# A two-layer hybrid decoder step on one core: the first half of the tokens goes through the output projection and four feed-forward tiles inside the first mixer's scan

## The chip, the cores and the metric

One NeuronCore of a Trainium2 chip. The metric is the device time of one execution in microseconds (us), the median of several runs. PE is TensorE (matmuls), PEld its weight loads, DVE VectorE, ACT ScalarE, POOL GpSimd, SP the queue that issues nearly all DMAs.

## The reference, cut to what matters

544 tokens (512 of one prompt and 8 short sequences of 4) pass two layers of width 1024. Layer 0 has two mixers side by side, an RG-LRU (a gated linear recurrence) and an RWKV-7 time mixing (a matrix state per head, updated token by token); layer 1 has HGRN2. Behind each stands a feed-forward block.

```
p = rmsnorm(x) @ w_in_ab
out_a = gelu(p[gate]) * rg_lru(conv(p[u]))
S = S*w_t - (S kk_t)(kk_t a_t)^T + v_t k_t^T      # for each token, each of 8 heads
o_t = S r_t;  out_b = (groupnorm(o) + bonus) * g
x = x + concat(out_a, out_b) @ w_out_ab
xf = rmsnorm(x)
x = x + (silu(xf @ ffn_gate) * (xf @ ffn_up)) @ ffn_down
```

## The kernel before, in words

Activations lie transposed: 128 features on the partitions, the 544 tokens along the row. A product in float32 is made of three matmuls in a shorter format (fp32r): the high part of the weight by the high part of the activation, high by low, and low by high. So each weight block of 128 x 512 is loaded (`wf`, 256 KB), its high part copied by ACT (`wh`, L202) and its low part subtracted by DVE or POOL (`wl`, L205). `weights` (L196 on) does this from pools of 2 `wf` and 3 `wh`/`wl` buffers. One output column of 128 features needs 8 k-tiles, so 2 blocks and 24 matmuls for a half of 272 tokens (`dense_steps`), and both halves use the blocks while they are there.

Mixer 0 ends with the scan of the RWKV part: 16 chunks of 32 tokens, each a chain of three small groups of products (tile `ch`): the state by W, copied out by DVE (`rhs`, L827); that by the inverse Yt, copied out by four DVE instructions into the two Z tiles (L842); these by TM, added to the decayed state by DVE (L850); then the chunk's outputs (`ops`). Between the three groups `fill(HOP[i])` takes a number of steps from a list of generators, `self.work`: a step is one dense matmul. The list holds `recurrent()`, the four RG-LRU column pairs with their gates (tile `gate`), and later `lead(3)`, which begins the output projection of three columns for tokens 0 to 255 (`SPLIT`). `PLAN` is an order written by hand: `c` one chunk, `s` one step of the sample group (tiles rpss, opss, dpss), `g`/`h` the two halves of a groupnorm of 128 tokens, `l` the lead, `f` n fill steps, `d` empty the list. The scheduler of the language keeps this order by priorities: the chain is put first (`first()`), weights 400 places early; within an engine everything then runs in the order built.

After the scan `out_proj0` finishes the output projection, five columns in a mixed order with the weights kept in two extra pools (`wo`, `wo2`), three columns in the common way; then `ffn(0, ...)` runs 22 tiles of gate and up in groups of 8, 8 and 6, each followed by the 8 down columns of its group. The eighth input of the projection, `oa[3]`, is the last that the recurrent part delivers.

Of the kernel before, what the change touches and what calls it, by code (L numbers as in the profile page):

```python
# [20 lines left out]
D = 1024  # L21
KT = 8
# [14 lines left out]
WC = 4  # L37
FREE = 'r3'
# [90 lines left out]
class Build:  # L129
    def __init__(self, nc, tc, ins, outs, dbg=None):  # L130
# [10 lines left out]
        self.normed = set()  # L141

# [192 lines left out]
    def mixer0(self):  # L335
# [22 lines left out]
        kp = self.open("keep", side="right")  # L358
# [81 lines left out]
        Zt = m0.tile([128, NCH, 2, CH], F32, name="Zt")  # L440
        NTt = m0.tile([128, 2, NCH, CH], F32, name="NTt")
# [23 lines left out]
        def proj_begin(j):  # L465
            X = m0.tile([128, SEQ + 7 * NB + 3], F32, tag="X", name="X", bufs=XB)
# [6 lines left out]
        def proj_end(j, out, X):  # L473
            nc.gpsimd.tensor_copy(shift_sb[:, j, :], X[:, SEQ:NT + 1:4])
            d = m0.tile([128, SEQ + 7 * NB], F32, tag="d", name="d", bufs=DB)[:, :NT]
# [329 lines left out]
        def scan():  # L805
# [15 lines left out]
            for c in range(NCH):  # L821
# [13 lines left out]
                with first():  # L835
# [3 lines left out]
                    for e in range(2):  # L839
                        for par in range(2):  # L840
                            q = quad(par, e)
                            nc.vector.tensor_copy(zc[par][q, e::2], cu[q])  # L842
# [23 lines left out]
        def groupnorm(o, n, blk):  # L866
            assert self.gated
            self.normed.add(blk)
            with tc.high_priority(offset=GN_PRIO):
                yield from normalise(o, n, blk)  # L870

# [116 lines left out]
        def rglru(i, before):  # L988
            UX = m0.tile([128, SEQ + 7 * NB + 3], F32, tag="X", name="UX", bufs=XB)
# [19 lines left out]
            cf = m0.tile([128, NX], F32, tag="d", name="cf", bufs=DB)  # L1009
# [8 lines left out]
            gg = m0.tile([128, SEQ + 7 * NB], F32, tag="d", name="gg", bufs=DB)[:, :NT]  # L1018
# [49 lines left out]
        cat, ww0, ps0 = [], [], []  # L1068
        H0, H1 = slice(0, SPLIT), slice(SPLIT, NT)

        def lead(n):
            assert {0, 1} <= self.normed
            wo = (self.open("wo", side="right"), (2, 2 * n - 2))
            cat.extend(actp.tile([128, 2, NT], F32R, tag="a", name="cat") for _ in range(8))
            for j in range(3):
                self.hilo(cat[j], oa[j])
            for j in range(4):
                self.hilo(cat[3 + j], bon[j], H0)
            for m in range(n):
                ww0.append(self.column(I["w_out_ab"][m], 0, KT, wo if m else None))  # L1080
            for m in range(n):
# [606 lines left out]
```

## Time and profile before

| what | value |
|---|---|
| median of 3 runs | 1540.75 us (1539.14 to 1542.7) |
| the profiled execution | 1541.22 us, its span 1539.4 us |
| PE busy | 1465.2 us, 95% of the span, 13872 matmul records |
| DVE, ACT, POOL busy | 860.2, 552.5, 418.3 us |
| DMA | 133.86 MB |

A row of a timeline is: start, duration in us, engine, line, operation, output<-input, shapes, count, and in brackets how long the engine stood idle before it and what ended that. A row of waits is: who, waited for whom, total us, times, longest. PEclk is the granted clock of TensorE as a share of full speed. The times of the trace count from the start of the span.

### The profile page before, as it was taken

To read this page: it belongs to the slowest core of one execution; us is meant where nothing else is said; L and a number is where in the kernel's file an instruction comes from. 1 tells how busy PE (TensorE), PEld (TensorE's weight loads), DVE (VectorE), ACT (ScalarE), POOL (GpSimd) and SP (SyncE) were. 2 spreads that over 40 slices of the span, in tenths; PEclk is the share of its full clock that TensorE was granted. 3 is DMA by queue.
4 is the path that set the end of the run, shared out by engine and by line. 5 is a ranking of instruction groups with operands and counts; after the bars stand their busy time and mean duration, and the time that the engine had idled before them with its cause. 6 is when DMAs were issued, how large, how long until landed. Compare 5 with 4: busy or idle time off the path is not lost.

```text
span 1539.4 us, 33537 instructions
## 1 busy us (share of the span) xinstructions
PE 1465.2 (95%) x13872; PEld 1408.7 (92%) x13872; DVE 860.2 (56%) x1618; ACT 552.5 (36%) x997; POOL 418.3 (27%) x540
## 2 busy tenths in 40 slices
PE   6967888779999999999999999999999999999998
PEld 6857777669999999999999999999999999999997
DVE  7777555785544344334576667666674433444444
ACT  5634234354433233223352333333453322332224
POOL 3664535542110011001133434444431100110010
PEclk9978989889999999999999999999999999999999
DMA  4224311122232322322231232322242222223221
GB/s 158 70 71 104 105 38 36 49 80 93 83 96 83 90 89 84 96 83 91 85 120 58 85 98 85 106 87 90 97 124 90 89 86 87 90 90 90 84 75 59
DMA packets 92010, 133.86 MB, mean 87 GB/s; under 512 B 28976, under 2 KB 34864, under 8 KB 91728
## 3 DMA queue, kind: packets, MB, share of 16 engines
q1 hardware_dynamic: 91856, 131.71, 27.2%
q8 instruction: 109, 1.79, 0.5%
q14 instruction: 45, 0.37, 0.1%
HBM read 120.65 MB, written 11.02 MB: 86 GB/s over the span
## 4 chain that ended last, share of the span: by engine, by line
PE 84%; DVE 7%; ACT 3%; issue 2%; DMA 2%; POOL 1%; SPq 1%; DVEq 0%; POOLq 0%; ACTq 0%
PE acc L171 74%; PE lv L171 2%; PE ops L171 1%; PE ch L171 1%; DVE Z L842 1%; DVE t L571 0%; PE ds L171 0%; PE tr L1503 0%; DVE W L528 0%; PE nps L171 0%; DVE wl L205 0%; DMA S<-rS 0%; DMA x<-xT 0%; DMA wd<-down 0%; DVE Pd L653 0%
## 5 line engine op out<-in xcount | busy, mean ns | idle before, releaser
L171 PE MATMUL acc<-xg,wh 128*128 128x272 f32 x4544 | 888.1, 293 | 11.7 <-ACT xg L262 7.2
L171 PEld LDWEIGHTS acc<-xg,wh 128*128 128x128 f32 x4544 | 721.7, 191 | 21.7 <-ACT xg L262 7.5
L171 PE MATMUL acc<-xg,wl 128*128 128x272 f32 x2272 | 653.1, 293 | 0.2 <-DVE wl L205 0.2
L202 ACT ACTIVATE wh<-wf 128x512 fp32r<-128x512 f32 (+1 forms) x404 | 250.8, 621 | 655.8 <-PE acc L171 544.3
L171 PEld LDWEIGHTS acc<-xg,wl 128*128 128x128 f32 x2272 | 429.1, 190 | 4.9 <-issue 1.3
L205 DVE TENSOR_TENSOR wl<-wf,wh 128x512 fp32r<-128x512 f32 (+1 forms) x373 | 267.1, 716 | 192.2 <-ACT wh L202 166.2
L1207 POOL TENSOR_TENSOR S<-S,rstd 128x272 f32<-128x272 f32 x88 | 74.3, 845 | 645.3 <-ACT S L1206 645.2
L171 PE MATMUL acc<-h,wh 128*128 128x272 f32 x1280 | 236.9, 288 | 0.0
L171 PEld LDWEIGHTS acc<-h,wh 128*128 128x128 f32 x1280 | 198.0, 188 | 0.0
L171 PE MATMUL acc<-h,wl 128*128 128x272 f32 x640 | 176.7, 287 | 0.0
L171 PEld LDWEIGHTS acc<-h,wl 128*128 128x128 f32 x640 | 118.1, 188 | 0.0
L1210 DVE TENSOR_TENSOR hh<-acc,S 128x272 f32<-128x272 f32 x88 | 38.9, 442 | 127.2 <-PE acc L171 125.3
L171 PE MATMUL acc<-cat,wh 128*128 128x272 f32 (+2 forms) x512 | 100.2, 295 | 2.7 <-ACT wh L202 2.7
L171 PEld LDWEIGHTS acc<-cat,wh 128*128 128x128 f32 x512 | 82.7, 194 | 3.5 <-ACT wh L202 3.1
L1206 ACT ACTIVATE S<-t 128x272 f32<-128x272 f32 x88 | 37.8, 431 | 123.4 <-DVE t L1205 123.4
L1227 DVE TENSOR_TENSOR x<-acc,x 128x272 f32<-128x272 f32 x80 | 35.0, 439 | 83.3 <-PE acc L171 83.0
L1205 DVE TENSOR_TENSOR t<-acc,rstd 128x272 f32<-128x272 f32 x88 | 38.7, 441 | 70.7 <-PE acc L171 70.6
L171 PE MATMUL acc<-cat,wl 128*128 128x272 f32 (+2 forms) x256 | 74.2, 296 | 2.0 <-POOL wl L205 1.0
L280 POOL TENSOR_TENSOR ssq<-ssq,sq 128x544 f32<-128x544 f32 x33 | 46.5, 1410 | 93.4 <-ACT sq L279 93.0
L1477 POOL TENSOR_TENSOR K<-K,G 128x256 f32<-128x256 f32 (+1 forms) x48 | 39.8, 828 | 78.3 <-PE lv L171 78.3
L205 POOL TENSOR_TENSOR wl<-wf,wh 128x512 fp32r<-128x512 f32 x31 | 41.3, 1334 | 40.7 <-ACT wh L202 40.4
L171 PEld LDWEIGHTS acc<-cat,wl 128*128 128x128 f32 x256 | 49.2, 194 | 2.8 <-POOL wl L205 1.4
(341 smaller groups left out, 1506.9 us busy)
## 6 DMA issues: line engine op xcount, KB each, us to landing
wf<-gate SPq DMA_DIRECT2D x88, 256.0 KB
wf<-up SPq DMA_DIRECT2D x88, 256.0 KB
wf<-down SPq DMA_DIRECT2D x72, 256.0 KB
wf<-w_in_c SPq DMA_DIRECT2D x64, 256.0 KB
wf<-w_in_ab SPq DMA_DIRECT2D x44, 256.0 KB
x<-xT SPq DMA_DIRECT2D x16, 272.0 KB
wf<-w_out_ab SPq DMA_DIRECT2D x16, 256.0 KB
S<-hS SPq DMA_DIRECT2D x8, 512.0 KB
```

What stands on the lines that cost most here:

```text
L171: return self.seq(self.nc.tensor.matmul(out, lhsT, rhs, start=start, stop=stop, skip_group_check=True), chain)
L202: nc.scalar.activation(wh[:, :n], wf[:, :n], AF.Copy)
L205: eng.tensor_tensor(wl[:, :n], wf[:, :n], wh[:, :n].bitcast(F32), OP.subtract)
L280: eng.tensor_tensor(self.ssq, self.ssq, t, OP.add)
L842: nc.vector.tensor_copy(zc[par][q, e::2], cu[q])
L1205: nc.vector.tensor_tensor(t[:, c], ps, rs()[:, c], OP.mult)
L1206: nc.scalar.activation(S[:, c], t[:, c], AF.Silu)
L1207: nc.gpsimd.tensor_tensor(S[:, c], S[:, c], rs()[:, c], OP.mult)
L1210: nc.vector.tensor_tensor(hh[:, c], ps, S[:, c], OP.mult)
L1227: nc.vector.tensor_tensor(x[:, c], ps, x[:, c], OP.add)
L1477: PTT(kv[:, :, 0], kv[:, :, 0], g2[:, :, 1, None].to_broadcast([128, m, b]), OP.mult)
```

## The change

The first half of the tokens (0 to 255) now goes as fill work through the whole output projection and the first four of the 22 feed-forward tiles (`PAIRS`), in `first_half()`, which joins the list after the eleventh chunk. Its first two columns (`EARLY`) leave out the last k-tile until `oa[3]` is there. What is not done by the end of the scan is done in `d0`, before the second half of the last groupnorm. `second_half` then takes tokens 256 to 543 through the same projection and the same four tiles, with all these weights loaded again, and from there both halves together. The weight loads outside the first two columns go in turn through the old pool (3 of 5) and a new one, `h0` (2 of 5), with 1 `wf` and 2 `wh`/`wl` buffers. The down products run in two groups (12 and 10 tiles) instead of three. Of the chain's four copies two go to ACT. Every second `wl` subtraction in the scan (it was every one) is POOL's. The sample group's steps and the groupnorms have other places in `PLAN`.

```diff
-LO = (3, 1)
+LO = (3, 2)
-PLAN = 's1 f30 c1 c1 s1 c1 s1 c1 s1 c1 s1 g0 c1 s1 c1 s1 c1 h0 s1 c1 s1 c1 s1 s1 c1 c1 s1 g1 c1 s1 c1 s1 c1 h1 g2 s1 c1 s1 l3 c1 c1 h2 f20 d0'
+PLAN = 's1 f30 c1 c1 s1 s1 c1 s1 s1 c1 s1 c1 s1 g0 s1 c1 s1 c1 s1 h0 c1 s1 c1 s1 g1 c1 s1 s1 c1 h1 s1 s1 c1 l0 c1 g2 c1 c1 c1 h2 c1 g3 c1 d0 h3'
-HOP = (8, 7, 7)
+HOP = (9, 10, 9)
...
     def column(self, src, k0, kn, pool=None):
-        return [(k, self.weights(src, k0 + k, min(WC, kn - k), pool)) for k in range(0, kn, WC)]
+        out = []
+        for k in range(0, kn, WC):
+            own = pool
+            if self.h0 and own is None:
+                self.turn += 1
+                if self.turn % 5 < 2:
+                    own = (self.h0, (1, 2))
+            out.append((k, self.weights(src, k0 + k, min(WC, kn - k), own)))
+        return out
...
                             q = quad(par, e)
-                            nc.vector.tensor_copy(zc[par][q, e::2], cu[q])
+                            copy(e, zc[par][q, e::2], cu[q])
...
+        def first_half():
             assert {0, 1} <= self.normed
+            self.close("rg", "join")
+            hp = self.h0 = self.open("h0", side="right")
+            cat = half["cat"] = [actp.tile([128, 2, NT], F32R, tag="a", name="cat") for _ in range(8)]
+            for j, src in enumerate([*oa[:3], *bon, oa[3]]):
+                self.hilo(cat[j], src, H0)
+            xs = half["x"] = [hp.tile([128, SPLIT], F32, name=f"xh{m}") for m in range(KT)]
+            for m in range(KT):
+                nc.sync.dma_start(xs[m], I["xT"][:, m, H0])
...
+            early = [(self.column(I["w_out_ab"][m], 0, KT, (self.wp, self.wbufs)), self.bank()) for m in range(EARLY)]
+            for ww, ps in early:
+                yield from self.run(None, acts, None, ww=ww, ps=ps, ks=range(KT - 1))
+            for m in range(KT):
...
+                if m < EARLY:
+                    yield from self.run(None, acts, ev, ww=early[m][0], ps=early[m][1], ks=(KT - 1,))
+                else:
+                    yield from self.run(I["w_out_ab"][m], acts, ev)
+                xg.append(self.scaled_half(hp, x, "ln_ffn0", m, ssq, SPLIT))
+            rs = half["rs"] = self.rstd_half(hp, ssq, SPLIT)
+            half["h"] = []
+            for ft in range(PAIRS):
+                yield from self.gate_up(hp, ft, [xg], [rs], half["h"])
...
+    def gate_up(self, hp, ft, xgs, rss, out, pool=None):
...
+        wg = self.column(self.i["gate0"][ft], 0, KT)
+        for c, xg, rs in zip(cuts, xgs, rss):
+            def evg(ps):
+                nc.vector.tensor_tensor(t[:, c], ps, rs(), OP.mult)
+                nc.scalar.activation(S[:, c], t[:, c], AF.Silu)
+                nc.gpsimd.tensor_tensor(S[:, c], S[:, c], rs(), OP.mult)
+            yield from self.run(None, [(a[:, 0], a[:, 1]) for a in xg], evg, ww=wg)
+        wu = self.column(self.i["up0"][ft], 0, KT)
...
+    def second_half(self, half):
...
+        for m in range(KT):
+            x = self.x[m][:, H1]
...
+            go(self.run(I["w_out_ab"][m], acts, ev))
+            xg1.append(self.scaled_half(hp, x, "ln_ffn0", m, ssq, n1))
+        rs1 = self.rstd_half(hp, ssq, n1)
+        h1 = []
+        for ft in range(PAIRS):
+            go(self.gate_up(hp, ft, [xg1], [rs1], h1))
...
+        for last, kn, pool in ((False, PAIRS + 8, self.act_a), (True, FT - PAIRS - 8, None)):
+            full = []
+            for ft in range(k0 + len(hs), k0 + kn):
+                own = self.act_a if last and len(full) < LENT else pool
+                go(self.gate_up(hp, ft, [half["xg"], xg1], [half["rs"], rs1], full, own))
```

Where instructions stand now, at three places. On PE, the fill between the first and the second product of a chunk (`acc` is a dense product, `xg` the recurrent part's input, `cat` the projection's, `rhs` by `Yt` the second product), before:

```order
L171 MATMUL jps<-join,Zt 32x16 x32
L171 MATMUL acc<-xg,wh 128x272
L171 MATMUL acc<-xg,wl 128x272
L171 MATMUL acc<-xg,wh 128x272 x2
L171 MATMUL acc<-xg,wl 128x272
L171 MATMUL acc<-xg,wh 128x272 x2
L171 MATMUL acc<-xg,wl 128x272
L171 MATMUL ch<-rhs,Yt 32x64 x8
```

and in the fourteenth chunk of the changed kernel:

```order
L176 MATMUL ch<-Z_2138,W_246 32x64
L176 MATMUL acc<-cat,wl 128x256
L176 MATMUL acc<-cat,wh 128x256 x2
L176 MATMUL acc<-cat,wl 128x256
L176 MATMUL acc<-cat,wh 128x256 x2
L176 MATMUL acc<-cat,wl 128x256
L176 MATMUL acc<-cat,wh 128x256 x2
L176 MATMUL ch<-rhs,Yt 32x64 x8
```

Nine matmuls of the first half's projection stand where eight of the recurrent part stood.

On ACT, around the fifth and sixth chunk (`uc` and `cf` belong to the recurrent part, `q` and `o` to a groupnorm, `Zs` to the sample group), before:

```order
L878 ACTIVATE q<-o 128x512
L793 ACTIVATE join<-jps 128x128
L1041 ACT_TABLE_LOAD
L1041 ACTIVATE uc<-uc 128x544
L202 ACTIVATE wh<-wf 128x512
L1011 ACTIVATE cf<-UX,vec 128x568
L962 ACTIVATE Zs_2181<-sps 32x2x64 x2
```

and in the changed kernel, a little earlier in the scan, since the sample group has moved:

```order
L207 ACTIVATE wh<-wf 128x512
L1055 ACT_TABLE_LOAD
L1055 ACTIVATE uc<-uc 128x544
L781 ACTIVATE Z_2136<-ch 32x2x64
L781 ACTIVATE Z_2140<-ch 32x2x64
L1025 ACTIVATE cf<-UX,vec 128x568
L872 ACTIVATE o<-ops 128x512
L892 ACTIVATE q<-o 128x512
L807 ACTIVATE join<-jps 128x128
L781 ACTIVATE Z_2133<-ch 32x2x64
L781 ACTIVATE Z_2137<-ch 32x2x64
```

The chain's copies (`Z<-ch`) now stand in ACT's queue between the table loads, the groupnorm and the weight copies.

On SP, the DMA issues at the end of the scan (`rS_p` stores the final state, which waits for the last chunk), before:

```order
L201 DMA wf<-w_out_ab 128x512 x3
L864 DMA rS_p<-Z_2130 64x256
L201 DMA wf<-w_out_ab 128x512
L864 DMA rS_p<-Z_2134 64x256
L201 DMA wf<-w_out_ab 128x512
L1111 DMA h_o<-h_sb 128x36
L201 DMA wf<-w_out_ab 128x512 x2
```

and in the changed kernel:

```order
L206 DMA wf<-w_out_ab 128x512 x7
L206 DMA wf<-gate 128x512
L878 DMA rS_p<-Z_2133 64x256
L878 DMA rS_p<-Z_2137 64x256
L206 DMA wf<-w_out_ab 128x512
L206 DMA wf<-gate 128x512
L206 DMA wf<-up 128x512
L206 DMA wf<-gate 128x512 x2
L206 DMA wf<-up 128x512 x2
```

The loads of the first half's last columns and of its first gate tile stand ahead of the stores, the rest of its weights behind them.

More of the change, by code (lines that the diff above doesn't have):

```diff
@@ L37 @@
 WC = 4
+PAIRS = 4
+LENT = 2
+EARLY = 2
 FREE = 'r3'
@@ L1099, in mixer0 @@
             elif k == "l":
-                self.work.append(lead(n))
+                self.work.append(first_half())
             elif k == "d":
@@ L1121, in mixer0, with run @@
-        self.hilo(cat[7], oa[3])
         for j in range(4):
-            self.hilo(cat[3 + j], bon[j], H1)
+            self.hilo(half["cat"][j if j < 3 else 7], oa[j], H1)
+        for j in range(4):
+            self.hilo(half["cat"][3 + j], bon[j], H1)
         self.lo_pool = 0
-        return cat, ww0, ps0
-    def late_pools(self):
+        self.close("keep")
+        return half
+    def run(self, src, acts, evac, k0=0, ww=None, ps=None, ks=None):
+        ww = ww or self.column(src, k0, len(acts))
+        n = acts[0][0].shape[-1]
+        ps = ps if ps is not None else self.bank()
+        prev = None
+        for kb, (wh, wl) in ww:
+            for k in range(min(WC, len(acts) - kb)):
+                w = slice(k * 128, (k + 1) * 128)
+                if ks and kb + k not in ks:
+                    continue
+                for q, (l, r) in enumerate(((wh, 0), (wh, 1), (wl, 0))):
+                    prev = self.order(prev, self.mm(ps[:, :n], l[:, w], acts[kb + k][r],
+                                                    start=(kb + k == 0 and q == 0),
+                                                    stop=(kb + k == len(acts) - 1 and q == 2), chain=True))
+                    yield
+        if evac:
+            evac(ps[:, :n])
@@ new lines, in bank, with scaled_half @@
+    def bank(self):
+        self.na += 1
+        if self.wide and self.na % 7 > 2:
+            return self.ms.tile([128, 512], F32, tag="m", name="acc")
+        return self.acc.tile([128, 512], F32, tag="acc", name="acc", bufs=3)
+    def scaled_half(self, pool, x, g, m, ssq, n):
+        nc = self.nc
+        if m == 0:
+            nc.scalar.activation(ssq, x, AF.Square)
+        else:
+            own = pool is self.h0
+            t = (pool if own else self.sqp).tile([128, n if own else NT], F32, tag="sq", name="sqh", bufs=2)[:, :n]
+            nc.scalar.activation(t, x, AF.Square)
+            nc.gpsimd.tensor_tensor(ssq, ssq, t, OP.add)
+        a = pool.tile([128, 2, n], F32R, name=f"xg{m}")
+        self.hilo_scaled(a, x, self.v(g, m))
+        return a
@@ new lines, in rstd_half, with get @@
+    def rstd_half(self, pool, ssq, n):
+        nc = self.nc
+        r = pool.tile([128, n], F32, name="rsh")
+        done = []
+        def get():
+            if not done:
+                ps = self.ms.tile([128, 512], F32, tag="m", name="nps")
+                self.mm(ps[:, :n], self.ones, ssq)
+                nc.scalar.activation(r, ps[:, :n], AF.Sqrt, bias=self.eps, scale=1.0 / D)
+                nc.vector.reciprocal(r, r)
+                done.append(1)
+            return r
+        return get
@@ L1655, in build @@
             B.dr = dr
[L1656 to L1660 removed]
+            half = B.mixer0()
+            xg = B.second_half(half)
             if stage >= 3:
```

156 lines of the change are left out of this document (75 added, 81 removed).

## The prediction

> **What bounds the kernel now.** I read the page first: PE is busy 95% of the span, so the question is where the other 5% lies. The table of windows answers it. I cut it at the second product of the scan's first chunk and of its last, whose rows in the timeline of PE are these:
>
> ```profile
> 182.20 0.43 PE L171 MATMUL ch<-rhs,Yt 32*32 32x64 f32 x16
> ...
> 328.12 0.65 PE L171 MATMUL ch<-rhs,Yt 32*32 32x64 f32 x16
> ```
>
> The page's first line, then the windows from there to the start of mixer 1 (columns: length, PE busy with its records, PEld, DVE, ACT and POOL busy, granted PE clock, DMA share, GB/s):
>
> ```profile
> span 1539.4 us, 33537 instructions
> ```
> ```profile
> 182.20:328.12 145.92, 118.63 (x1996) 96.69 (x1995) 97.43 (x246) 54.91 (x92) 66.11 (x85) 0.88 0.17 54
> 328.12:356.92 28.80, 24.09 (x193) 22.29 (x193) 22.20 (x46) 16.60 (x31) 8.15 (x7) 0.82 0.50 166
> 356.92:807.70 450.78, 450.77 (x3588) 450.09 (x3588) 216.58 (x358) 151.22 (x260) 61.73 (x68) 1.00 0.28 88
> ```
>
> From 356.92 on PE never waits and runs at full clock: there only the number of matmul columns counts. In the scan it waits 145.92 - 118.63 = 27.3 us, and its 118.63 us of work ran at 0.88 of the clock, so 0.12 x 118.63 = 14.2 us more are lost. In the 28.8 us behind it 4.7 us are waits and 0.18 x 24.09 = 4.3 us clock. Together 50.5 us are lost on PE between the scan's start and the dense stage. What PE waits for in the scan (total, times, longest):
>
> ```profile
> PE ch L171 <- DVE Z L842: 13.9, 11, 3.4
> PE rpss L171 <- DMA S<-rS: 3.7, 1, 3.7
> PE ch L171 <- DVE rhs L827: 3.0, 3, 1.5
> PE tps L895 <- POOL o L889: 1.8, 1, 1.8
> PE gate L171 <- ACT tr L1033: 1.8, 1, 1.8
> PE gate L171 <- DVE S L984: 1.2, 1, 1.2
> PE ch L171 <- DVE Z L850: 1.2, 1, 1.2
> ```
>
> Half of it is one wait: the third product of a chunk waits for the four copies of L842. It comes in bursts, and a burst costs twice, as two places in the timeline show with the windows that hold them:
>
> ```profile
> 220.51 0.42 PE L171 MATMUL ch<-rhs,Yt 32*32 32x64 f32 x16 [1.50 <-DVE rhs L827]
> ...
> 223.44 1.12 PE L171 MATMUL ch<-Z,TM 64*64 64x64 f32 x16 [1.44 <-DVE Z L842]
> ...
> 270.95 1.12 PE L171 MATMUL ch<-Z,TM 64*64 64x64 f32 x16 [3.41 <-DVE Z L842]
> ```
> ```profile
> 220.00:230.00 10.00, 7.40 (x138) 5.98 (x142) 9.74 (x26) 3.60 (x8) 5.97 (x9) 0.61 0.11 35
> ...
> 270.00:280.00 10.00, 8.81 (x120) 7.50 (x121) 6.75 (x25) 1.26 (x2) 2.51 (x3) 0.66 0.06 12
> ```
>
> DVE is full (9.74 of 10 us) when the chain needs it, PE waits, and then PE's granted clock is 0.61 and 0.66.
>
> **The change part by part. PE's own work: nothing.** Splitting the tokens 256 and 288 instead of 272 and 272 keeps the columns; the pitch decides whether it keeps the time. The dense stretch in the chain of work, and three matmuls each of 256 and of 288 columns:
>
> ```profile
> 394.96 399.55 PE acc L171 x3192
> ```
> ```profile
> 346.02 0.40 PE L171 MATMUL acc<-cat,wh 128*128 128x256 f32 x2
> ...
> 346.73 0.40 PE L171 MATMUL acc<-cat,wh 128*128 128x256 f32 x2
> ...
> 356.92 0.42 PE L171 MATMUL acc<-cat,wh 128*128 128x288 f32 x2
> ...
> 357.32 0.43 PE L171 MATMUL acc<-cat,wh 128*128 128x288 f32 x2
> ```
>
> 272 columns take 399.55 / 3192 = 0.125 us, 256 take (346.73 - 346.02) / 6 = 0.118, 288 take (357.32 - 356.92) / 3 = 0.133: 0.251 for a pair either way. The second weight load of PE hides behind the matmuls as the first does. So all matmuls are as many and as long as before, and the change can win only from the 50.5 us, and lose only by new waits. That is the frame of the sum.
>
> **Cover in the scan.** Each chunk now holds 9, 10 and 9 fill matmuls instead of 8, 7 and 7. Before the third product that is 3 x 0.125 = 0.38 us more cover. And two of the four copies go to ACT. What the four cost on DVE, and two like them on ACT:
>
> ```profile
> 184.16 1.19 DVE L842 COPY Z<-ch 32x128 f32<-32x128 f32 x4
> ```
> ```profile
> 227.64 0.55 ACT L962 ACTIVATE Zs<-sps 32x128 f32<-32x128 f32 x2 [5.10 <-PE sps L171]
> ```
>
> Two and two side by side end after 0.60 instead of 1.19 us. Per wait that is between 0.38 us (ACT comes too late to help) and 0.97 us; below zero if ACT is itself held, which is a rival. With 11 waits the ends are 4.1 and 10.7; I take 6.6, since ACT is busy only 54.91 of 145.92 us but is in order. The wait on the first copy loses 0.13 x 3 = 0.4, that on L850 0.2. Sum: **-7.2**.
>
> The steps of the sample group go two to a chunk at the start, so their products (the same ones) stand where fewer fills did; their wait for S (3.7) stays, because its load still stands behind the 16 Z loads on SP's queue. POOL gives half of the `wl` subtractions to DVE: some 8 of them in the scan at 0.69 (row below), 5.5 us, against 16 x 0.60 = 9.6 us of copies that leave DVE. I cost both at nothing beyond the waits counted; the cover is the fills, and if it fails the price is the last rival's.
>
> **Clock.** 14.2 us hang on about four bursts. I let one fall: **-3.5**; the ends are 0 and 14.2. The Trainium skill, TensorE: Matmul & The Clock Gate, section "HAM oscillation — how this bites in real kernels", allows PE gaps up to about 3.4 us before the clock drops. The trace differs: 1.50 and 1.44 us close together were enough for 0.61. By that rule only the waits of 3.7 and 3.4 us would matter and this term would be 0, the time 3.5 us longer.
>
> **A new wait at the end of the recurrent part.** `first_half` needs its eighth input (oa[3]) in the last k-tile of its first column. In the program order that product now stands 42 fills after the last gate product. What the chain from there took before:
>
> ```profile
> 327.46 0.72 PE L171 MATMUL gate<-uc,gates 128*128 128x272 f32 x2 [1.78 <-ACT tr L1033]
> ```
> ```profile
> 345.10 0.72 DVE L258 TENSOR_TENSOR cat<-v,cat 128x544 fp32r<-128x544 f32 x1
> ```
>
> From 328.2 to 345.8 are 17.6 us. PE has 42 x 0.118 = 5.0 us of fills, and about 3.5 us of the chunk's own products, in front. Before, groupnorm 3 lay between; without it the chain is shorter. Between 0 and 9 us of stall; PE is in order, so the scan's products behind it wait too. I take **+4**.
>
> **Behind the scan.** The 4.7 + 4.3 = 9.0 us go: PE now has 91 + 192 matmuls of the first half in the queue while the last groupnorm runs. **-9.0**; the ends are -9.0 and 0. New is the appetite for weights. A block of 512 weight columns now serves 12 matmuls before the next is needed, 12 x 0.118 = 1.42 us or 12 x 0.133 = 1.59, where a full column of two halves gives it 24 x 0.125 = 3.0. This goes on for 283 / 12 = 23.6 and then 384 / 12 = 32 blocks: 84 us. One buffer's turn, from the issue on SP to the end of the subtraction, alone and beside other loads:
>
> ```profile
> 399.19 0.33 SPq L201 DMA_DIRECT2D wf<-gate  x1
> ...
> 401.98 0.63 ACT L202 ACTIVATE wh<-wf 128x512 fp32r<-128x512 f32 x1 [1.05 <-DMA wf<-gate]
> 402.64 0.69 DVE L205 TENSOR_TENSOR wl<-wf,wh 128x512 fp32r<-128x512 f32 x1 [2.18 <-ACT wh L202]
> ```
> ```profile
> 342.32 1.10 SPq L201 DMA_DIRECT2D wf<-w_out_ab  x2
> ```
> ```profile
> 346.49 0.63 ACT L202 ACTIVATE wh<-wf 128x512 fp32r<-128x512 f32 x1 [0.48 <-DMA wf<-w_out_ab]
> ```
> ```profile
> 347.15 1.19 DVE L205 TENSOR_TENSOR wl<-wf,wh 128x512 fp32r<-128x512 f32 x1 [0.26 <-DMA x<-xT]
> ```
>
> Alone it is 403.33 - 399.19 = 4.14 us; the second load of 342.87 took until about 347.84, 5.0 us. Two of every five blocks pass through the one `wf` buffer of the new pool, so five blocks take 2 x 4.14 = 8.3 us or 2 x 5.0 = 10.0: 1.66 to 2.0 us a block, more than PE's 1.42 or 1.59. A POOL subtraction makes it longer still:
>
> ```profile
> L205 POOL TENSOR_TENSOR wl<-wf,wh 128x512 fp32r<-128x512 f32 x31 | 41.3, 1334 | 40.7 <-ACT wh L202 40.4
> ```
>
> Against it stands a lead of 8 blocks (3 + 2 converted, 2 + 1 arriving), 8 x 1.5 = 12 us. So 55.6 x 1.66 - 84 - 12 is below zero: no stall; 55.6 x 2.0 - 84 - 12 = 15 us of stall. I take **+4**, nearer the lone turn, since the first of the two stretches begins with the lead full.
>
> On SP the half-width x loads and some ten weight loads now stand ahead of the two stores of the prompt's state, which wait for the last chunk, and the loads behind these are held until then; the lead of 8 blocks covers that. ACT gets two more table loads (square root and SiLU, for the first half by itself); they delay an evacuation, and PE has two more columns, 48 x 0.118 = 5.7 us, before it needs that bank.
>
> The other edits have one answer: 32 more loads (0.63 us on ACT and 0.69 on DVE each) lie beside PE's work except as just priced; two groups of down products instead of three have the same matmuls; the pools that move to the other side carry the same tiles, and PE's order is the same up to the first chunk.
>
> **Sum.** -7.2 - 3.5 + 4 - 9.0 + 4 = -11.7 us. The profiled execution took 1541.22 us; that gives 1529.5. It lies 0.5 above the median of the runs, so the forecast for the median is **1529** (its own range 1521 to 1538).
>
> **The rivals.** *The waits close (18%).* If ACT's half of the copies is always in time (10.7 instead of 6.6), the clock stays up (14.2 instead of 3.5) and neither stall comes (8 us less), the time is 1529 - 4 - 10.7 - 8 = 1506; with half of the clock's part 1513. For it: every burst but S begins with a wait that the chain's cover can shorten. Against: the 3.4 us wait is far beyond 0.97.
>
> *The weights become the bound (18%), slower.* The place is the two half-width stretches, the mechanism the one-buffer pool at 2 of 5 blocks. At a turn of 5.0 us the stall is 15 us, which eats the gain of 11.7 + 4 = 15.7; from there on the kernel is slower. At 5.5 us it is 55.6 x 2.2 - 96 = 26 us: 1529 - 4 + 26 = 1551. For it: 5.0 us was seen when two loads and the x loads ran together, and in the half-width stretches loads are never alone. Against: the lead, and the new pool itself.
>
> *The clock falls in every block (4%).* If the short waits for weights held PE's clock at 0.66 through the 84 us, 84 x 0.5 = 43 us come on top: 1572. Here two waits of under 1 us on DVE's `wl` left it at 1.00:
>
> ```profile
> PE acc L171 <- ACT wh L202: 2.7, 1, 2.7
> PE acc L171 <- POOL wl L205: 1.0, 2, 0.9
> PE acc L171 <- DVE wl L205: 1.0, 2, 0.7
> ```
> ```profile
> 350.00:360.00 10.00, 9.04 (x70) 8.46 (x69) 5.14 (x11) 2.79 (x7) 0.00 (x0) 1.00 0.35 133
> ```
>
> The Trainium skill tells of such a loop on the same page and in the same section, compute per tile shorter than the wait for the next one and a cold clock in each tile; the window above speaks against it.
>
> *The chain grows (15%).* The recurrent part's DVE work now ends by chunk 12, not 15, and ACT's copies queue behind its table loads and behind `wh` conversions that wait for PE. If that costs the 11.7 us, the time is that of before, 1541. For it: DVE had 97.43 us of work in those 145.92. Against: 9.6 us leave it. It also covers that the change does nothing.
>
> **How the numbers follow.** 45% for the forecast, 18, 18, 4 and 15 for the others. A measurement of this kernel tells 0.2% (3.1 us) from no change: faster is below 1537.7, slower above 1543.8. The forecast's case is faster but for 0.03, the first rival wholly; the weights' rival is slower but for 0.03, the cold blocks wholly; of the last rival a third falls to each side. Faster: 0.42 + 0.18 + 0.05 = 0.65; slower: 0.15 + 0.04 + 0.05 = 0.24; the rest 0.11. The range reaches into the first rival and into that of the weights: 1513 to 1549.
>
> **What would show it.** Right: the window from the first chunk's second product to the last one's near 146 us with some 90 more fill matmuls in it, PE's wait on L842 near 7 us, no clock under 0.9 in the stretch behind the scan. Wrong: waits of PE on `wh`, `wl` or weight loads of more than 10 us between the scan and the first full pair; or a stall of over 8 us on the eighth input; or a PE wait for ACT's copies larger than the 13.9 us of now.

## The result and the profile after

| | us | 95% interval of the ratio |
|---|---|---|
| kernel before, median of 4 | 1541.03 | |
| changed kernel, median of 4 | 1563.39 | |
| ratio | 1.0145 | 1.0120 to 1.0169 |

The change makes the kernel 22 us slower; the forecast was 12 us faster, with a range that ended at 1549. The profiled execution has a span of 1563.9 us (before 1539.4). The scan again runs from the second product of its first chunk to that of its last:

```profile
183.21 0.43 PE L176 MATMUL ch<-rhs,Yt 32*32 32x64 f32 x16
...
354.35 0.43 PE L176 MATMUL ch<-rhs,Yt 32*32 32x64 f32 x16
```

The windows for the scan, for the half-width stretch behind it, and from the first product of mixer 1's `d` to the end (columns as before: length, PE busy with its records, PEld, DVE, ACT, POOL, granted PE clock, DMA share, GB/s):

```profile
183.21:354.35 171.14, 138.58 (x2097) 113.45 (x2096) 104.59 (x243) 79.35 (x153) 68.62 (x85) 0.85 0.21 66
354.35:439.50 85.15, 73.86 (x592) 71.18 (x592) 57.94 (x100) 46.89 (x94) 29.21 (x29) 0.98 0.47 150
829.14:1563.90 734.76, 725.57 (x6429) 705.63 (x6428) 396.92 (x727) 246.64 (x460) 182.06 (x215) 0.99 0.27 88
```

The last of them in the kernel before:

```profile
807.63:1539.40 731.77, 723.95 (x6429) 704.38 (x6428) 395.87 (x728) 243.54 (x458) 183.58 (x216) 1.00 0.28 88
```

The scan has 101 more PE records, work of some 13 us at full clock (138.58 x 0.85 against 118.63 x 0.88), but it is 25.2 us longer. Put side by side, with the clock's loss as (1 - granted clock) x PE busy:

| lost on PE, us | before | after |
|---|---|---|
| scan, idle | 27.3 | 32.6 |
| scan, clock | 14.2 | 20.8 |
| behind the scan, idle + clock | 4.7 + 4.3 | 11.3 + 1.5 |
| sum | 50.5 | 66.2 |

The frame was that only these 50.5 us could be won. They grew by 15.7 instead. The last window adds 3.0 us and the start of the scan 1.0, which is within what that start varies between traces whose code is the same up to there (182.27 us in e6, 184.23 in e20, both below). What PE waits for in the scan now:

```profile
PE ch L176 <- ACT Z L781: 9.9, 7, 4.9
PE rpss L176 <- DMA S<-rS: 6.3, 1, 6.3
PE tps L909 <- POOL o L903: 4.3, 1, 4.3
PE ch L176 <- DVE st L901: 3.0, 1, 3.0
PE dpss L176 <- POOL vx L990: 2.9, 3, 1.3
PE sps L176 <- ACT Zs L976: 1.6, 1, 1.6
PE ch L176 <- DVE Z L864: 1.2, 1, 1.2
PE ch L176 <- DVE rhs L841: 1.0, 2, 0.8
```

Read in two groups. The chain's own waits (copies, `Z` of L864, `rhs`) fell from 13.9 + 1.2 + 3.0 = 18.1 to 12.1 us. The waits that come from the sample group and the group norms (S, `o`, `st`, `vx`, `Zs`) rose from 3.7 + 1.8 + 0.6 = 6.1 to 18.1 us; the last of the three before is

```profile
PE sps L171 <- ACT Zs L962: 0.6, 1, 0.6
```

Those had been costed at nothing. Eight of the runs below keep the changed kernel's places and its 28 fills a chunk (e1, e6, e8, e12, e13, e16, e17, e20). In their traces the second group is 16.7 to 19.5 us, so its rise repeats. The first group is 11.9 to 15.8 us (without e13, which has a stall of its own) and the clock's loss 14.8 to 19.4: the 20.8 above is the highest of the nine.

And behind the scan, where nothing was to wait:

```profile
PE acc L176 <- ACT wh L207: 5.0, 3, 3.1
PE acc L176 <- ACT xg L275: 2.1, 1, 2.1
PE acc L176 <- DVE bonus L921: 1.2, 1, 1.2
PE ch L176 <- ACT Z L781: 1.1, 1, 1.1
PE acc L176 <- POOL wl L210: 0.8, 1, 0.8
PE acc L176 <- DVE wl L210: 0.5, 2, 0.3
```

The four copies of a chunk, in the timelines of VectorE and ScalarE at one chunk:

```profile
202.64 0.58 DVE L783 COPY Z<-ch 32x128 f32<-32x128 f32 x2 [2.57 <-PE ch L176]
```
```profile
203.31 0.55 ACT L781 ACTIVATE Z<-ch 32x128 f32<-32x128 f32 x2 [1.51 <-DVE Z L783]
```

ScalarE's two start when VectorE's two are done, and are released by them. From 202.64 to 203.86 are 1.22 us, as long as four on VectorE (1.19). The forecast's 0.60 us needed them side by side. The Trainium skill, PSUM — Partial Sum Buffer, section "PSUM bank collisions raise a hardware error", says that two engines on one bank must be kept apart within a quadrant of 32 partitions, and that different quadrants may be used at the same time. These copies lie in four different quadrants, so by that rule the chip would not need the wait, and it would be one that the build puts in; no run here lets them go at once.

### The profile page after: what moved, and what is told of

Same layout as the page of the kernel before. It is cut to its first block, busy times and chain, and to the rows that moved or that the text cites. A ratio compares the mean times of both kernels' runs of the same rounds, so it can differ in the third digit from the quotient of the medians.

```text
span 1563.9 us, 33790 instructions
## 1 busy us (share of the span) xinstructions
PE 1475.9 (94%) x13872; PEld 1415.2 (90%) x13872; DVE 864.5 (55%) x1616; ACT 591.3 (38%) x1090; POOL 423.7 (27%) x549
## 4 chain that ended last, share of the span: by engine, by line
PE 72%; DMA 2%; DVE 2%; ACT 1%; issue 1%; POOL 0%; DVEq 0%; ACTq 0%; POOLq 0%
PE acc L176 66%; PE lv L176 2%; DMA wf<-w_out_ab 1%; PE ops L176 1%; DMA wf<-gate 1%; DVE wl L210 0%; PE ds L176 0%; PE tr L1613 0%; ACT wh L207 0%; PE nps L176 0%; PE opsm L176 0%; PE d L176 0%; PE opsq L176 0%; PE dss L176 0%; DMA wf<-up 0%
## 5 line engine op out<-in xcount | busy, mean ns | idle before, releaser
L176 PE MATMUL acc<-xg,wh 128*128 128x272 f32 (+2 forms) x4544 | 895.5, 294 | 16.1 <-ACT xg L275 9.4
L176 PE MATMUL acc<-xg,wl 128*128 128x272 f32 (+2 forms) x2272 | 659.2, 293 | 1.1 <-POOL wl L210 0.8
L207 ACT ACTIVATE wh<-wf 128x512 fp32r<-128x512 f32 (+1 forms) x436 | 269.8, 622 | 646.1 <-PE acc L176 477.9
L176 PE MATMUL acc<-h,wh 128*128 128x272 f32 (+2 forms) x1280 | 238.5, 288 | 0.0
L176 PE MATMUL acc<-h,wl 128*128 128x272 f32 (+2 forms) x640 | 179.8, 287 | 0.0
L1317 POOL TENSOR_TENSOR S<-S,rstd 128x272 f32<-128x272 f32 x44 | 37.6, 855 | 330.8 <-ACT S L1316 330.8
L1216 POOL TENSOR_TENSOR S<-S,rsh 128x256 f32<-128x256 f32 (+1 forms) x44 | 35.9, 817 | 283.8 <-ACT S L1215 283.8
L1320 DVE TENSOR_TENSOR hh<-acc,S 128x272 f32<-128x272 f32 x44 | 19.4, 441 | 62.9 <-PE acc L176 62.9
L276 DVE SCALAR_TENSOR_TENSOR xg<-x,vec,xg 128x544 fp32r<-128x544 f32 (+1 forms) x32 | 33.8, 1058 | 16.5 <-ACT xg L275 16.2
L1316 ACT ACTIVATE S<-t 128x272 f32<-128x272 f32 x44 | 19.0, 431 | 62.0 <-DVE t L1315 62.0
```

The source lines that it names most:

```text
L176: return self.seq(self.nc.tensor.matmul(out, lhsT, rhs, start=start, stop=stop, skip_group_check=True), chain)
L207: nc.scalar.activation(wh[:, :n], wf[:, :n], AF.Copy)
L276: nc.vector.scalar_tensor_tensor(act[:, 1], src, g, act[:, 0].bitcast(F32), op0=OP.mult, op1=OP.subtract)
L1216: nc.gpsimd.tensor_tensor(S[:, c], S[:, c], rs(), OP.mult)
L1316: nc.scalar.activation(S[:, c], t[:, c], AF.Silu)
L1317: nc.gpsimd.tensor_tensor(S[:, c], S[:, c], rs()[:, c], OP.mult)
```

## The experiments

All have five rounds beside the kernel before on the same chip, and each ratio is to that. Where a run is compared with the changed kernel, the two ratios are compared.

**Copies.** In the changed kernel back to VectorE (e1); in the kernel before, half of them to ScalarE (e2).

```diff
-                            copy(e, zc[par][q, e::2], cu[q])
+                            nc.vector.tensor_copy(zc[par][q, e::2], cu[q])
```

> The changed kernel with the four copies of each chunk back on VectorE, all else as changed. If the copies on two engines run side by side, as the forecast had it (0.60 instead of 1.19 us), this loses about 11 x 0.6 = 6.6 us against the changed kernel: about 1570 us. If the two engines read the one PSUM tile one after the other (0.58 + 0.09 + 0.55 us in the trace, as long as four on VectorE) and ScalarE's pair besides hangs on ScalarE's queue (the waits of 4.9 and 1.5 us), this gains: PE's waits for ACT of 9.9 us become waits for DVE of about 5, and the clock burst behind the 4.9 us wait goes: 1555 to 1560 us. If it stays within 2 us of 1563, the copies are not where the time went.

1565.54 us, 1.0167 (1.0154 to 1.0180): no difference from 1.0145 (1.0120 to 1.0169) that can be told. The copies are not where the time went, and the gain of 3 to 8 us that was expected of copies one after the other did not come.

> The kernel before with two of the four copies of each chunk on ScalarE, that one line alone. Side by side: the 13.9 us that PE waits for the copies fall to about 7 and some clock comes back: 1531 to 1536 us. One after the other: the wait stays as long or grows where ScalarE is held by its own queue: 1541 to 1547 us, and the third product's waits name ACT.

1545.62 us, 1.0039 (1.0027 to 1.0051): slower. PE's wait for the copies grew from 13.9 us to

```profile
PE ch L171 <- ACT Z L767: 20.8, 14, 3.1
```

in the scan. So one after the other, and by itself the split costs 6 us; in the changed kernel e1 shows no such price.

**Places of the sample group and the norms**, in the kernel before (e4; it leaves out the two stores of the prompt's state, since the plan has one step too few).

```diff
-PLAN = 's1 f30 c1 c1 s1 c1 s1 c1 s1 c1 s1 g0 c1 s1 c1 s1 c1 h0 s1 c1 s1 c1 s1 s1 c1 c1 s1 g1 c1 s1 c1 s1 c1 h1 g2 s1 c1 s1 l3 c1 c1 h2 f20 d0'
+PLAN = 's1 f30 c1 c1 s1 s1 c1 s1 s1 c1 s1 c1 s1 g0 s1 c1 s1 c1 s1 h0 c1 s1 c1 s1 g1 c1 s1 s1 c1 h1 s1 s1 c1 c1 g2 c1 c1 l3 c1 h2 c1 f20 d0'
```

> The kernel before with the changed kernel's places for the sample group's steps and for the group norms (two sample steps to a chunk in four places, all sixteen by the twelfth chunk); the fills, the copies and the place of the output projection's first part stay. Forecast's theory (the places cost nothing): 1541 us within 2. Rival (the places are what costs): the waits of the changed kernel for the sample group's S, o, vx and st appear here too (6.3 + 4.3 + 2.9 + 3.0 us where the kernel before had 3.7 + 1.8 + 0 + 0), some 11 us of waits and 3 to 6 us of clock: 1550 to 1558 us.

1540.99 us, 1.0014 (1.0005 to 1.0024). The waits for `o` and `st` did not come; S, `vx` and `Zs` (with 0.5 for its load) are 2.7, 2.6 and 1.1, together 6.4 us against 6.1. The places alone are nearly free. Two things came with them: the chain's waits fell to 14.8 us without a fill more, and the clock's loss in the scan is 20.6 us.

**Columns cut at 256 and 288**, in the kernel before, in the first feed-forward layer (e7).

```diff
-            c = slice(h * HF, (h + 1) * HF)
+            c = ((slice(0, SPLIT), slice(SPLIT, NT)) if self.uneven else (slice(0, HF), slice(HF, NT)))[h]
```

> The kernel before with the first feed-forward layer's columns cut at 256 and 288 instead of 272 and 272, nothing else. Forecast's theory (a pair takes 0.251 us either way): 1541 us within 1. Rival, from the pitches of the changed kernel's dense stretch (0.1200 + 0.1322 = 0.2522 against 2 x 0.1252 us, over 1584 pairs): 2.9 us longer, 1543.9 us.

1540.17 us, 1.0003 (0.9993 to 1.0013): free.

**Fills in a chunk.** In the changed kernel 8, 7, 7 (e5) and 11, 12, 11 (e18); in the kernel before 9, 8, 8 (e15).

```diff
-HOP = (9, 10, 9)
+HOP = (8, 7, 7)
```

> The changed kernel with 8, 7 and 7 fill matmuls in a chunk instead of 9, 10 and 9, all else as changed. Forecast's theory (more fills are more cover for the chain): 11 x 0.38 = 4 us are lost, about 1567 us. Rival (the fills are not cover but load: they bring the first half's and the recurrent part's work on VectorE, ScalarE and GpSimd in front of the chain's steps, so the waits for o, vx, st and S come from them): PE's waits in the scan fall below the 32.6 us of the changed kernel by 5 us or more and the time is 1556 to 1560 us.

> The changed kernel with 11, 12 and 11 fill matmuls in a chunk instead of 9, 10 and 9. With 8, 7 and 7 it took 10 us more than with 9, 10 and 9. If that is a slope (fills are cover for the chain), 6 more gain 5 to 8 us: 1555 to 1558 us. If fills only move work from behind the scan into it, the time stays within 2 us of 1563. If the recurrent part's supply runs out before the first half begins, or its work on VectorE comes in denser, chunks without cover cost more: 1567 us and above.

> The kernel before with 9, 8 and 8 fill matmuls in a chunk instead of 8, 7 and 7, nothing else. Cover: 0.125 us more before the first copy and as much again before the third product, over 11 to 14 waits: 1537 to 1539 us, with PE's wait for the copies near 11 us. If the recurrent part's fills only run out three steps earlier (the last chunks then stand without fills), the wait grows there again: 1541 to 1545 us.

e5: 1573.60 us, 1.0216 (1.0195 to 1.0237). e18: 1557.74 us, 1.0119 (1.0103 to 1.0134). With 22, 28 and 34 fills the changed kernel takes 2.16, 1.45 and 1.19% more than the kernel before: more fills help it, and from 22 to 28 by more than the 4 us of the forecast's cover. The scan and the first 85 us behind it, of e5 and of e18:

```profile
183.70:335.46 151.76, 123.05 (x2008) 96.55 (x2007) 91.48 (x226) 65.12 (x127) 58.39 (x77) 0.89 0.17 52
335.46:420.46 85.00, 66.83 (x512) 63.16 (x512) 49.40 (x88) 46.35 (x90) 32.32 (x29) 0.90 0.46 139
```
```profile
182.00:352.13 170.13, 135.59 (x2151) 111.90 (x2150) 109.81 (x250) 84.86 (x163) 72.85 (x90) 0.91 0.24 73
352.13:437.13 85.00, 76.75 (x598) 74.32 (x598) 57.30 (x101) 46.83 (x92) 25.65 (x25) 0.96 0.48 150
```

With few fills PE loses less in the scan (28.7 us idle against 32.6) and much more behind it (18.2 against 11.3). That they do so as cover of the chain is not shown. Its own waits are 18.9 us with 22 fills, 12.1 with 28 and 21.0 with 34 (and 22.5 with the 40 of e21 below); in e18 the copies alone are

```profile
PE ch L176 <- ACT Z L781: 14.8, 10, 2.7
```

Idle time and clock together are 42.2, 53.4, 46.7 and 47.3 us in these four scans, and 24.9, 12.8, 11.3 and 7.9 us in the first 85 us behind them. What falls with more fills is the second number: half-width work done inside the scan is not left for the stretch that waits for weights. That this is why the time falls is read from these sums, not tried by itself.

e15 took 1546.93 us, 1.0052 (1.0038 to 1.0065), slower. Its scan holds 8 more records, not 48, and PE waits there for

```profile
PE ch L171 <- DVE rhs L827: 12.2, 8, 3.8
```

instead of 3.0: the recurrent part's supply runs out, and the last chunks stand bare. Fills help only while there are some.

**Pairs taken at half width**, two instead of four (e6: `PAIRS = 2`).

> The changed kernel with two instead of four gate-and-up pairs of the feed-forward layer taken at half width (their weights are loaded once again, 4 MB less traffic). If the half-width stretches starve for weights (PE's waits of some 11 us between the scan and the dense stretch), half of the feed-forward's share in them goes: 3 to 5 us faster than the changed kernel, 1558 to 1560 us. If the loss lies in the scan's order, the time stays within 2 of 1563 us.

1563.88 us, 1.0161 (1.0143 to 1.0179): no gain. The waits behind the scan stay (4.8 us for `xg`, 3.3 for `wh`): with half the pairs they are not fewer.

**Who subtracts.** All of `wl` in the scan on GpSimd (e8: `LO = (3, 1)`); all on VectorE from the first half on (e20); every second one on VectorE in the kernel before (e19: `LO = (3, 2)`). The edit of e20, in `first_half`:

```diff
             hp = self.h0 = self.open("h0", side="right")
+            self.lo_pool = 0
```

> The changed kernel with all subtractions for wl during the scan on GpSimd, as in the kernel before, instead of every second one. If VectorE's load in the scan is what delays the chain (some 8 subtractions of 0.69 us there), the scan's waits fall by about 3 us; behind the scan GpSimd's 1.33 us a block, close to PE's 1.42 us, then hold PE for some us more. Sum within 3 us of 1563 either way; the two windows tell which. If neither window moves by 2 us, where the subtraction stands does not matter.

> The changed kernel with all subtractions for wl on VectorE from the first half's start on (before that every second one on GpSimd as changed). In the trace of the changed kernel the loads on SyncE's queue waited 38.1 us in 15 places for GpSimd's subtraction (1.29 us each, up to 8.5 us with what stood ahead of it) and 18.7 us in 20 for VectorE's. If GpSimd holds the buffers, PE's waits for wh and wl behind the scan fall from 6.3 us to 2 or 3: 1556 to 1560 us. If VectorE, which then has 16 more of 0.69 us, holds the chain and the buffers instead: 1563 us and above.

> The kernel before with every second subtraction for wl during the scan on GpSimd instead of all of them, as the changed kernel has it. In the changed kernel all on GpSimd cost 6 us. If GpSimd's 1.33 us a block delays weights in the kernel before as well (PE waited 1.0 us for them there, and 2.7 for ScalarE's wh), this gains 1 to 3 us: 1537 to 1539 us. If VectorE's 5.5 us more delay the chain's copies instead, 1542 to 1546 us. Within 1 us of before, the share does not matter there.

e8: 1569.43 us, 1.0187 (1.0173 to 1.0202), 6 us slower, where the expectation allowed 3: GpSimd's `wl` (4.3) and `ssqh` (2.5) hold PE behind the scan. e20: 1561.69 us, 1.0139 (1.0125 to 1.0153), no difference that can be told, though the largest entry of SyncE's waits in the changed kernel (window 300 to 440) was

```profile
SPq L206 <- POOL wl L210: 38.1, 15, 8.5
```

A queue's long wait says who is last on that queue, not that it costs the kernel. e19: 1544.51 us, 1.0027 (1.0016 to 1.0039): in the kernel before GpSimd is the better place.

**The old scan, the first half behind it** (e10): the kernel before's `PLAN` with `l0` for `l3` and ending `h2 g3 d0 h3`, its `HOP`, and the copies on VectorE.

> The changed kernel with the scan as it was: the places of the sample group's steps and of the group norms, the fills (8, 7, 7) and the copies on VectorE as in the kernel before, and the first half put at the place where the output projection's first part was (behind the sixteenth step), so nearly all of it runs behind the scan. If the loss is the scan's new order, this is the time before plus only what the half-width stretch waits more (10.9 against 4.7 us): about 1547 us, with a scan of 146 us. If the half-width stretch's appetite for weights is the loss, that stretch is now 768 matmuls long with no scan beside the first 384, and waits 15 us or more: 1555 us and above. By the forecast's sum without the scan's gain and the eighth input's stall (-9 + 4) it would be 1536 us.

1558.86 us, 1.0123 (1.0105 to 1.0140). The scan is as expected, and the loss has moved behind it:

```profile
182.25:325.60 143.35, 117.87 (x1996) 95.31 (x1995) 96.85 (x248) 54.92 (x93) 57.03 (x76) 0.88 0.19 56
325.60:410.60 85.00, 70.00 (x534) 66.85 (x534) 54.22 (x99) 47.62 (x92) 31.87 (x30) 0.90 0.46 138
```
```profile
PE acc L176 <- ACT wh L207: 9.0, 7, 3.6
PE tps L909 <- POOL o L903: 5.6, 1, 5.6
```

The two rows count as far as mixer 1. Of the 15.0 us idle in the 85 us, 9.1 are for `wh` and `wl` and 5.6 for the last group norm. So the half-width stretch waits by itself, without the new scan.

**The scan's new order without second loads** (e14): the kernel before with the changed kernel's places, its fills (9, 10, 9), and `l3` behind the twelfth step.

> The kernel before with the changed kernel's order of the scan and its fills (9, 10, 9), but with the first part of the output projection, at full width and loaded once, begun behind the twelfth chunk's step instead of the first half; copies on VectorE, no second load. If more fills are cover (forecast's theory: 11 x 0.38 us and some clock), this gains 4 to 8 us on the kernel before: 1533 to 1537 us. If fills that come earlier only lengthen the scan by their own time, it stays within 2 us of 1541. If they bring the waits for o, st, vx and S with them, 1545 us and above.

1551.32 us, 1.0076 (1.0063 to 1.0090). Its waits in the scan, of the two groups:

```profile
PE ch L171 <- DVE Z L842: 7.6, 8, 1.4
PE ch L171 <- DVE rhs L827: 7.0, 5, 2.3
PE tps L895 <- POOL o L889: 5.8, 1, 5.8
PE dpss L171 <- POOL vx L976: 3.3, 3, 1.6
```

and behind the scan 11.2 us for `o` of the last group norm, whose cover was spent in the scan. So the new scan costs by itself too, here 12 us, the larger part of it behind the scan: inside, idle time and clock rose only from 41.5 to 45.7 us. The two prices (19 and 12) add to more than the 22 of the change. In e10 nearly all the half-width work stands behind the scan, in the changed kernel a part of it inside; that the two prices overlap for this reason was not tried.

**Hardly any loads** (e13, e16). Both leave out weight loads of the half-width stretches, those of the first half as well as the second loads: all products there use one column's weights (e13), or, behind the first two columns, the third's (e16). Both also take no other weights from the first half's pool (`self.turn % 5 < 0`). The lines of e16:

```diff
+            one = [(k, self.weights(I["w_out_ab"][EARLY], k, WC, (hp, (1, 2)))) for k in (0, WC)]
+            self.one = one
```
```diff
     def column(self, src, k0, kn, pool=None):
+        if self.one:
+            return self.one
```

> The changed kernel, which leaves out all weight loads of the two half-width stretches but one: every column of the output projection and of the four half-width pairs multiplies with the first column's weights, which stay in the first half's own buffers (the full-width stretch behind then has only the main buffers). What is left out is the work of some 64 loads: DMA, conversion on ScalarE, subtraction on VectorE or GpSimd. If the appetite for weights is the loss, PE's waits between the scan and the dense stretch fall from 10.9 to 3 us or less, and ScalarE and VectorE, which are freed in the scan too, shorten its waits: 1545 to 1554 us. If the loss is the order of the scan or work that PE has more of, the time stays above 1558 us.

> The changed kernel, which leaves out the weight loads of the two half-width stretches except those of its first two columns and of the third, whose weights all later half-width products use (the full-width stretch behind has only the main buffers). The first columns load as in the changed kernel, so the 15.1 us stall that the run with a single load had in the scan should be gone. If the appetite for weights is the loss, PE's waits behind the scan go from 10.9 us to below 3 and the scan's stay near 32: 1549 to 1555 us. If the same stall comes back at another place of the first column, the load itself is late there for a reason that the number of loads does not set: 1556 us and above.

e13 took 1558.21 us, 1.0122 (1.0108 to 1.0137), but its edit made a new stall of 15.1 us on the first column's `wh` in the scan, so it prices nothing. e16: 1554.14 us, 1.0085 (1.0071 to 1.0100). PE never waits behind the scan:

```profile
183.42:356.81 173.39, 136.28 (x2097) 110.67 (x2096) 104.41 (x245) 78.58 (x151) 66.25 (x83) 0.88 0.21 62
356.81:441.81 85.00, 84.96 (x707) 84.35 (x707) 36.62 (x76) 26.39 (x57) 15.66 (x20) 1.00 0.06 16
```

The loads left out cost about 0.6%, 9 us. They are more than the second loads: the kernel before has 32 blocks for these columns, e16 only 6. So the second loads by themselves were not priced. With all but these few gone the change still loses 13, and its scan is as bad as ever (37.1 us idle).

**Weight buffers** (e17): none in the first half's pool.

```diff
-                if self.turn % 5 < 2:
+                if self.turn % 5 < 0:
```

> The changed kernel without weight buffers in the first half's own pool: every block goes through the main pool's two wf and three wh and wl buffers. If the one wf buffer of the other pool, which takes two blocks of five, is what holds the order up (the mechanism of the forecast's rival), PE's waits for wh and wl behind the scan (6.3 us) shrink: 1556 to 1560 us. If more buffers are more lead whatever pool they are in, they grow by 5 us or more, also in the full-width stretch: 1568 us and above.

1594.70 us, 1.0353 (1.0336 to 1.0369). PE's waits for weights from the scan to mixer 1 are now

```profile
PE acc L176 <- ACT wh L207: 12.0, 15, 1.7
PE acc L176 <- POOL wl L210: 7.7, 9, 1.0
```

Without the one-buffer pool it takes 32 us more: its buffers are lead. Whether more buffers in it, or a smaller share of the blocks, would gain was not tried.

**Turn of the PSUM banks** behind the feed-forward layer (e12).

```diff
         self.close("ffn", "h0")
         self.h0 = None
+        self.na = 186
```

> The changed kernel with one number set behind the first feed-forward layer: the count by which dense products take their PSUM bank in turn (180 there, 186 in the kernel before), so that mixer 1 and all behind it take the banks as before. From the first product of mixer 1's d to the end the changed kernel took 734.8 us and the kernel before 731.8, with a stall of 1.1 us on xg at 1154.49 and slow clock behind it. If the turn of the banks moved that stall into place, the stretch is 731.8 us again and the time 1560.4 us. If not (buffers lie elsewhere, the queues stand otherwise), it stays at 734.8 and 1563.4 us.

1561.95 us, 1.0147 (1.0129 to 1.0165): the time does not tell 3 us. The stretch does. The stall of the changed kernel, and the stretch of e12:

```profile
1154.49 0.39 PE L176 MATMUL acc<-xg,wh 128*128 128x272 f32 x1 [1.12 <-ACT xg L275]
```
```profile
828.91:1560.50 731.59, 723.74 (x6429) 704.18 (x6428) 398.25 (x728) 243.62 (x458) 181.43 (x216) 1.00 0.29 88
```

Both kernels with the first half and the old turn (e12, e21) have 731.6 and 731.5 us there, all eleven others with the first half 733.9 to 736.1.

**All mended** (e21): fills 13, 14, 13, with the edits of e20 and e12.

> The changed kernel with 13, 14 and 13 fills in a chunk, all subtractions of the first half and what follows on VectorE, and the banks in their old turn behind the feed-forward layer. If the prices add (more fills: 6 more gained 4 to 5 us, the next 6 less, say 2 to 4; VectorE's subtractions about 1 to 2; the banks 3 in the stretch from mixer 1 on), this takes 1548 to 1553 us, and so is still 8 us or more above the kernel before. If the recurrent part's supply runs out before the first half may begin, chunks 9 to 12 stand without fills and it takes 1557 us or more. At 1541 us or less the split itself would cost nothing.

1546.78 us, 1.0048 (1.0035 to 1.0062), a little better than the sum of the prices.

```profile
185.95:357.74 171.79, 139.86 (x2176) 117.48 (x2175) 111.34 (x262) 87.72 (x167) 62.22 (x83) 0.89 0.26 76
357.74:442.74 85.00, 78.66 (x624) 76.54 (x623) 61.41 (x115) 49.05 (x96) 15.83 (x17) 0.98 0.50 152
```

Two thirds of the loss come back; 7 us stay. No version here beats the kernel before.

## Why the prediction was wrong

The step that failed is the one that put a price of nothing on the sample group's steps, "I cost both at nothing beyond the waits counted", and left the group norms' new places without a price: their waits rose by 12.0 us. With it failed "**-9.0**" for the stretch behind the scan, which with the +4 for weights was to gain 5 us and lost 3.8. The subtractions, the other of the "both", are not what failed: e8, with all of them back on GpSimd, still has 16.7 us of the sample group's and norms' waits. Term by term, from the two profiles:

| term | forecast | measured | by |
|---|---|---|---|
| chain's waits in the scan | -7.2 | -6.0 | 18.1 to 12.1 us |
| sample group and norms | 0 | +12.0 | 6.1 to 18.1 us |
| clock in the scan | -3.5 | +6.6 | 14.2 to 20.8 us |
| wait for the eighth input | +4 | +0.8 | `cat`, 0.6 + 0.2 us |
| behind the scan, with the weights | -9.0 + 4 | +3.8 | 9.0 to 12.8 us |
| from mixer 1 on | 0 | +3.0 | 731.8 to 734.8 us |
| PE's own work | 0 | about +2 | below |

Smaller waits of the scan (`gate`, `bonus`) fell by 1.6 us, and with the later start (1.0) the rows give 21.6 of the 24.5 us between the two spans. Some 3 us stay unexplained.

**Cover.** The size came near, by luck in good part. "Two and two side by side end after 0.60 instead of 1.19 us" fell with e2 and the rows above. The other half, the added fills, is not shown: e4 has 14.8 us of the chain's waits from the places alone, e10 has 14.8 with the old places, fills and copies, and e18 and e21, with still more fills, have 21.0 and 22.5.

**Sample group and norms.** e4 has the new places with 22 fills: 6.4 us. e5 has them too, with 22 fills: S 5.0, `vx` 2.6, `Zs` 0.6, in all 8.2. With 28 fills the changed kernel has 18.1 and e14, which has no first half, 5.8 + 3.3 and for S, its loads and `Zs` 2.3 + 1.2 + 1.6, in all 14.2. So the new places with 28 fills have it, in both kernels, and the new places with 22 do not. The old places with 28 fills were not run; with 25 (e15) S, its load and `Zs` are 3.4 us. A likely reason is that with denser fills the recurrent part's work on VectorE, ScalarE and GpSimd comes in front of the sample group's in fewer microseconds; that was not tried. It is no slope either: e18 has 5.8 for S, 1.8, 1.7 and 1.7 for `dpss` and `tps` and 1.3 for `Zs`, in all 12.3, and e21 9.0. Which steps meet at 28 fills stays open.

**Clock.** Two of the long waits are followed by a slow stretch:

```profile
270.86 0.63 PE L909 MATMUL tps<-ident,o 32*128 32x32 f32 x4 [4.30 <-POOL o L903]
...
331.74 1.12 PE L176 MATMUL ch<-Z,TM 64*64 64x64 f32 x16 [4.86 <-ACT Z L781]
```
```profile
270.00:280.00 10.00, 8.78 (x127) 7.81 (x127) 7.98 (x21) 2.52 (x7) 4.87 (x5) 0.57 0.08 29
...
330.00:340.00 10.00, 7.79 (x90) 6.41 (x90) 8.65 (x22) 4.57 (x10) 6.04 (x6) 0.67 0.15 44
```

The forecast let one burst fall, and new ones took its place. Their price is not settled by the waits: in the 10 us behind the wait for S the clock is 0.51 here, 0.82 in e6 and 0.71 in e20, after 6.25, 5.79 and 6.54 us. So the +6.6 of the table varies from trace to trace: it is the highest of the nine with 28 fills, and the others give +0.6 to +5.2. The Trainium skill, TensorE: Matmul & The Clock Gate, section "HAM oscillation — how this bites in real kernels", has the clock drop behind gaps of about 3.4 us, and waits of 4.30 and 4.86 us agree; the 10 us from 300, with 0.66 and no wait over 1.28 us, do not. The loop of cold blocks that it tells of did not come: with waits for weights of up to 3.1 us the half-width stretch has a clock of 0.98.

**Behind the scan.** "The 4.7 + 4.3 = 9.0 us go" holds if weights are nearly free: e16 has no idle time there at all. With the loads of the change it does not, and e10 shows that this needs no new scan. The rival of the weights named the place, and its price (15 to 26 us of stall) was too high for what the changed kernel shows there (`wh`, `wl` and `xg` 8.4 us); its mechanism, the one wf buffer at two blocks of five, is not borne out by e17: without that buffer PE's waits for weights grew. GpSimd's subtraction as the holder fell with e20, the number of pairs with e6. What the runs leave is lead for the weights: buffers (e17), and less half-width work left for this place (e5 and e10 leave more of it and lose more there, e18 and e21 less). In e14, where the fills behind the scan were no half-width work, the stretch lost its cover instead.

**PE's own work.** The uneven cut is free (e7). But 256 columns read from a tile of their own, 256 wide, are slower than from a slice of a 544 wide one. In e7, and then in the changed kernel:

```profile
433.41 0.40 PE L172 MATMUL acc<-xg,wh 128*128 128x256 f32 x2
...
434.82 0.67 PE L172 MATMUL acc<-xg,wh 128*128 128x288 f32 x4
```
```profile
502.15 0.40 PE L176 MATMUL acc<-xg,wh 128*128 128x256 f32 x2
...
505.03 0.43 PE L176 MATMUL acc<-xg,wh 128*128 128x288 f32 x2
```

1.41 us for 12 are 0.1175, 2.88 us for 24 are 0.1200 us each; over the 18 x 48 = 864 such products of the full-width pairs that is 2.2 us. In the changed kernel's own trace the same count from `cat`, a slice of a 544 wide tile, takes 0.118 us (358.48 to 362.03 us, 30 products), so it is not the kernel around it. Whether it is the width of the tile or where it lies was not tried.

**What would show it wrong.** None of the three alarms went off: waits for `wh`, `wl` and loads 6.3 us (bound 10), the eighth input 0.8 (8), ACT's copies 9.9 (13.9). They watched the new operations. The loss in the scan came in old ones that the change had only moved. Of the signs of being right, the window of the scan near 146 us failed (171.14) and the clock behind it held but for one place (0.98 over the stretch, 0.83 in the 10 us from 424, behind the wait of 3.1 us).

## What to carry to other kernels

Fill work is a finite supply. Moved under a chain, it can be missing from the place that it covered before (e14, e15), and where it has to be split it brings loads, conversions and evacuations of its own; sum the idle time and the clock of both places, before and after, and not the one that is to be filled. Halving the width of a weight-bound product halves the time that a block of weights has to arrive, so the buffers must be counted at the new width. And a step costed at nothing needs a row that shows its waits at its new place and with the new work around it, even if its instructions are the same.

## What was not expected of the hardware

The same number of columns costs 0.1175 us from a slice of a wide tile and 0.1200 us from a narrow tile of its own. And the turn in which PSUM banks were taken, shifted by one of seven before mixer 1 begins, goes with 3 us in the 732 us from there to the end, in two traces against eleven; the runs' times do not tell it. In the changed kernel's trace it is a wait of 1.12 us at 1154.49, a shorter one of 0.39 and a granted clock of 0.83 from 1154 to 1164.
